# A hybrid encoder layer: x loaded as column blocks and scaled there, its rows' squares taken beside the memory's keys

## The chip, the cores and the metric

One core of a Trainium2 chip runs the whole program in one launch. The metric is the device time of that launch in microseconds. The engines are TensorE (PE; its weight loads are PEld), VectorE (DVE), ScalarE (ACT), GpSimd (POOL) and SyncE (SP), which here only issues DMAs; POOL issues some too.

## What is computed

One encoder layer on x (1024 tokens by 1024), cut to the parts around the change:

```python
h = _rms(x, mix_norm_g)                    # x * rsqrt(mean(x*x) + eps) * g
p = h @ w_in                               # 1952 columns: 256 q, 128 kv, 32 rotary key, 3*512 Hyena
a_out = _mla(p[..., :256], p[..., 256:384], p[..., 384:416], ...)
kf = _hyena_filters(S, ...)                # a small sine net, a window, then a DFT
h_out = _hyena(p[..., 416:], conv_w, conv_b, kf, skip)
x = x + concat(_rms(a_out), _rms(h_out)) @ w_out
x = x + _mem_xattn(_rms(x, cross_norm_g), _rms(mem, mem_norm_g), w_mq, w_mkv, w_mo)
x = x + _hier_moe(...)
return _rms(x, final_norm_g)
```

The change concerns the first two lines, `_rms(x)` and its way into the projection.

## The kernel before

Precision is held by pairs: `split(hi, lo, src)` (L196) casts a tile to fp32r on ACT and subtracts that from the source on DVE, and `mm3` (L206 to L208) makes a product of two such pairs with three matmuls. A matmul contracts over partitions, so the projection needs x with its 1024 columns on partitions, eight blocks of 128, called hA (blocks 0 to 2) and hB (3 to 7), each as a high and a low tile.

The program is written as generators that are advanced in turn, and a scheduler then puts each engine's instructions in one fixed order; an instruction waits in its engine's queue, and all behind it wait with it.

- `spectra` (L286 and on) advances three generators until the filters' spectra are stored. `mem_side` normalises the 256 memory tokens and, for each of 16 column blocks of w_mkv, loads the weights (wm), splits them (wmh, wml), makes 24 matmuls of 256 columns (pmk) and stores the result to DRAM (kvd); later it folds w_mq and w_mo with keys and values. `filter_mlp` is the sine net of two layers (ph, u, h, hh; the cast of its result is h2h). `filters` makes for each of 2 x 8 token blocks a window (dec is the decay table, win the window, eo sums and differences on POOL, L362 and L363, split to eoh and eol), transforms them by DFT tables (ftab, loaded by POOL's DMAs; q1 and q2 are PSUM tiles) and combines them on DVE (L406, kts), which SP stores (Kd).
- `x_rows` comes in when all windows are made. It loads x by rows, eight tiles of 128 tokens (xt, L476), squares each on ACT with a sum (L482), makes the inverse root (`rstd`, L229 to L239: four small DVE operations, and the power on POOL), and scales the row tile by it on ACT (L486). The memory of these tiles was that of the window's tables, so SP's loads wait for the last window activation.
- `in_proj` (L494 and on) turns the rows: `turn_rows` transposes the eight blocks of one row tile on PE into PSUM (pt), and splits them from there into hA and hB. hB lies on memory of the filter transform. Then come twelve columns of 128 (order 8 to 11, then 0 to 7), 48 matmuls each into pu, then ACT (uc, L572) and DVE add the convolution of three taps, and the column is transposed back (pv). `weights` fetches a column's weights one ahead; POOL scales them by the norm's gain gx (L541), ACT casts them (L542), POOL subtracts (L543). From the third column on, the convolution of the finished columns runs between. The last 416 columns (q and kv) take wa, which `split_scaled` (L201, L202) scales and splits.

Tiles of x, of weights and of uc share a pool of eight buffers of 128 x 1024 (`x4`, tag x) and two more (tag u).

## Time and profile before

| | |
|---|---|
| median of 3 runs | 1499.66 us (1496.63 to 1503.1) |
| profiled execution | 1501.6 us, its span 1499.8 us |
| mean granted TensorE clock | 0.969 of full |
| PE / DVE / ACT / POOL busy | 1373.0 / 1034.5 / 701.7 / 498.9 us |

The span runs from the first instruction to the last. A timeline row gives start, duration, engine, line, operation, output and inputs with their shapes, how many equal instructions it joins, and in brackets how long the engine stood idle before it and what it waited for. "x16" in a timeline is one row for sixteen instructions; a DVE or ACT duration contains any time for which the instruction was held up after its start.

### The profile page before, as it was taken

What the parts mean: (1) busy time and instruction counts of PE and PEld (TensorE: products, weight loads), DVE (VectorE), ACT (ScalarE), POOL (GpSimd) and SP (SyncE); (2) the same over time, 40 slices, a digit from 0 to 9 for tenths busy, and PEclk for the clock granted to TensorE, in tenths of its full rate; (3) what the DMA queues carried; (4) which work ended last, traced back from release to release, by engine and by line L of the source; (5) the groups of instructions that cost most, each with busy time, mean ns of one, the idle gap of its engine ahead of it and who ended that gap; (6) DMA issues with size and microseconds to landing.
All of it is one profiled execution on the core that took longest, in us unless ns stands there. A gap on an engine that the chain in (4) does not pass through costs nothing. (4 is left out here: it accounts for less than half of the span.)

```text
span 1499.8 us, 19038 instructions
## 1 busy us (share of the span) xinstructions
PE 1373.0 (92%) x6702; PEld 1025.5 (68%) x6702; DVE 1034.5 (69%) x1755; ACT 701.7 (47%) x1035; POOL 498.9 (33%) x363
## 2 busy tenths in 40 slices
PE   8888988999898989899899999999998999999990
PEld 5777767877787876565555788887886555666660
DVE  7655455389888888456657776434475598899985
ACT  6647446322212224434444344322232687888973
POOL 1321143354433242666666200000001238443322
PEclk9999999999999999999999999999999999999996
DMA  7458776343684525000311421004567899999995
GB/s 266 141 172 298 267 265 224 111 141 130 220 267 154 171 84 168 2 15 1 116 47 43 127 94 57 0 1 169 195 232 253 277 343 362 331 327 331 332 329 216
DMA packets 103406, 272.95 MB, mean 182 GB/s; under 512 B 13162, under 2 KB 41002, under 8 KB 103182
## 3 DMA queue, kind: packets, MB, share of 16 engines
q1 hardware_dynamic: 88590, 222.16, 42.3%
q0 software_dynamic: 14720, 49.57, 11.6%
q8 instruction: 53, 0.87, 0.2%
q14 instruction: 43, 0.35, 0.1%
HBM read 225.83 MB, written 50.07 MB: 184 GB/s over the span
## 5 line engine op out<-in xcount | busy, mean ns | idle before, releaser
L196 DVE TENSOR_TENSOR wt<-raw,wt 128x1024 fp32r<-128x1024 f32 x180 | 214.7, 1217 | 28.1 <-ACT wt L196 25.8
L196 ACT CAST wt<-raw 128x1024 fp32r<-128x1024 f32 x180 | 185.2, 1048 | 20.1 <-PE pgu L208 9.8
L994 POOL TENSOR_TENSOR sums<-sums,e 128x1024 f32<-128x1024 f32 x56 | 134.0, 2393 | 77.2 <-ACT e L990 75.4
L990 ACT ACTIVATE e<-psc 128x1024 f32<-128x1024 f32 x64 | 65.6, 1025 | 85.2 <-PE psc L208 81.9
L950 DVE TENSOR_REDUCE cn<-ptop 128x1 f32<-128x1024 f32 x64 | 75.7, 1211 | 41.2 <-PE ptop L949 40.8
L206 PE MATMUL pgu<-wt,xh 128*80 128x512 f32 x240 | 97.9, 408 | 0.0
L207 PE MATMUL pgu<-wt,xh 128*80 128x512 f32 x240 | 95.5, 398 | 0.0
L208 PE MATMUL pgu<-wt,xh 128*80 128x512 f32 x240 | 95.2, 397 | 0.0
L1835 POOL DMA_INDIRECT acc<-y,tab x28 | 51.2, 1827 | 118.9 <-ACT y L1832 100.7
L206 PE MATMUL psc<-xq,xk 97*128 97x512 f32 (+1 forms) x128 | 56.5, 441 | 11.3 <-ACT e L990 4.5
L1772 POOL DMA_INDIRECT xg<-h3d,tab x32 | 47.6, 1487 | 48.4 <-PE pxt L212 29.3
L999 PE MATMUL po<-e,V 128*64 128x512 f32 x256 | 58.5, 598 | 0.0
L362 POOL TENSOR_TENSOR eo<-win 128x512 f32<-128x512 f32 x16 | 23.8, 1488 | 87.8 <-DVE win L360 87.8
L206 PE MATMUL pw<-woh,ot 128*128 128x512 f32 x128 | 50.6, 395 | 1.6 <-DVE xr L1141 1.3
L207 PE MATMUL psc<-xq,xk 97*128 97x512 f32 (+1 forms) x128 | 52.0, 407 | 0.0
L208 PE MATMUL psc<-xq,xk 97*128 97x512 f32 (+1 forms) x128 | 52.0, 406 | 0.0
L233 POOL TENSOR_TENSOR fr<-fr0v,mhalf 128x1 f32<-128x1 f32 x4 | 2.3, 579 | 149.2 <-DVE fr0v L231 131.1
L572 ACT ACTIVATE uc<-pu,cw 128x1024 f32<-128x1024 f32 x12 | 14.5, 1209 | 78.6 <-PE pu L208 78.6
L206 PE MATMUL pcs<-kh,chh 128*128 128x512 f32 x128 | 50.4, 394 | 0.0
L207 PE MATMUL pw<-wol,ot 128*128 128x512 f32 x128 | 49.9, 390 | 0.0
L208 PE MATMUL pcs<-kh,chl 128*128 128x512 f32 x128 | 49.9, 389 | 0.0
L207 PE MATMUL pcs<-kl,chh 128*128 128x512 f32 x128 | 49.8, 389 | 0.0
(539 smaller groups left out, 4127.3 us busy)
## 6 DMA issues: line engine op xcount, KB each, us to landing
raw<-in_w_exp SPq DMA_DIRECT2D x192, 512.0 KB
tab<-in_t_cfwd POOLq DMA_DIRECT2D x32, 512.0 KB
ftab<-in_t_fwd POOLq DMA_DIRECT2D x16, 768.0 KB
wm<-in_w_mkv SPq DMA_DIRECT2D x16, 512.0 KB
Kd<-kts SPq DMA_DIRECT2D x16, 512.0 KB
kt<-Kd SPq DMA_DIRECT2D x32, 256.0 KB
tab<-in_t_inv SPq DMA_DIRECT2D x32, 256.0 KB
w<-in_w_hy SPq DMA_DIRECT2D x12, 512.0 KB
```

The lines of the kernel that those rows point to most:

```text
L196: return self.nc.scalar.copy(hi, src).ins, self.nc.vector.tensor_tensor(lo, src, hi.bitcast(F32), op=ALU.subtract).ins
L206: mm(out, lh, rh, start=start, stop=False)
L207: mm(out, lh, rl, start=False, stop=False)
L208: mm(out, ll, rh, start=False, stop=stop)
L362: nc.gpsimd.tensor_tensor(t[:, 0], win[:, :512], win[:, 512:], op=ALU.add)
L572: nc.scalar.activation(y, pu, AF.Identity, scale=cw[:, c, 1:2], bias=cw[:, c, 3:4])
L950: nc.vector.tensor_reduce(cn[:, i, r:r + 1], ps, axis=AX.X, op=ALU.max, negate=True)
L990: nc.scalar.activation(e, ps, AF.Exp, scale=SCALE)
L994: nc.gpsimd.tensor_tensor(sums, sums, e, op=ALU.add)
L999: nc.tensor.matmul(po[par * 64:par * 64 + 64], V[:, kt, v], e[:, par * 512:(par + 1) * 512], start=kt == 0, stop=kt == NT - 1, skip_group_ ...
L1772: return nc.gpsimd.indirect_dma_start(out=x, out_offset=None, in_=self.h3d, in_offset=bass.IndirectOffsetOnAxis(ap=tok, axis=0), bounds_ch ...
L1835: scat = nc.gpsimd.indirect_dma_start(out=self.acc, out_offset=bass.IndirectOffsetOnAxis(ap=to, axis=0), in_=y, in_offset=None, bounds_che ...
```

## The change

1. The squares of x's rows move into `mem_side`: in the loop over the 16 memory columns, from c = 5 to 12, one row tile of x is loaded (xq, one more SP DMA of 512 KB each) and, two columns later, squared on ACT. All eight sums go into one tile, and one `rstd` follows at the loop's end (xr_r). `spectra` advances its generators in the same proportion, and `x_rows` two steps at a time.
2. `x_rows` loads x a second time, now as eight column blocks from a transposed copy `xT`, which the host lays out among the inputs. The eight roots per partition are spread over all partitions: DVE multiplies an identity by them (dg), two matmuls in fp32 with a tile of ones sum that over partitions into PSUM (L485), ACT copies it to SBUF (xrb, L486).
3. Each column block is scaled by gx on ACT (L491) and by the roots on POOL (L492), and split into hA or hB from SBUF. Transposes, `turn_rows` and its splits from PSUM are gone.
4. The weights are no longer scaled: L541's multiplication on POOL is gone (ACT's cast is now L541, POOL's subtraction L542), and wa takes `split`, four of 832 columns, in place of eight `split_scaled` of 416.

The diff's core:

```diff
 # spectra
             for step, _ in enumerate(self.filters()):
-                if step % 2 == 0 and not self.made:
+                if not self.made:
+                    if step % 2 == 0:
+                        next(side, None)
                     next(side, None)
-                if not self.made or next(side, self) is not self:
-                    if not self.made:
-                        next(side, None)
                     continue
                 if rows is None:
+                    for _ in side:
+                        pass
                     rows = self.x_rows()
+                next(rows, None)
                 next(rows, None)
...
 # x_rows
+        for k in range(8):
+            t = self.x4([P, S], F32, "xt")
+            nc.sync.dma_start(t, a["xT"][k])
             self.xt.append(t)
...
+        dg, r = self.x4([P, NT, P], F32, "dg", "u"), self.x4([P, S], F32, "xrb", "u")
+        with tc.high_priority():
+            nc.vector.memset(one, 1.0)
+            nc.vector.tensor_tensor(dg, self.ident[:, None, :].broadcast_to([P, NT, P]), self.xr_r[:, :, None].broadcast_to([P, NT, P]), op=ALU.mult)
+            for n in range(2):
+                nc.tensor.matmul(pr[:, n * 512:(n + 1) * 512], one, dg[:, 4 * n:4 * n + 4].rearrange("p i t -> p (i t)"), start=True, stop=True)
+            nc.scalar.copy(r, pr)
...
+        for k in range(8):
+            nc.scalar.activation(self.xt[k], self.xt[k], AF.Identity, scale=self.gx[:, k:k + 1])
+            nc.gpsimd.tensor_tensor(self.xt[k], self.xt[k], r, op=ALU.mult)
+            if k < 3:
+                self.split_x(*self.hA, k, k)
+            if k % 2:
+                yield
...
 # in_proj, weights(c)
-                if "W" in POOL:
-                    nc.gpsimd.tensor_tensor(w, w, self.gx[:, :, None].broadcast_to([P, 8, P]), op=ALU.mult)
-                    nc.scalar.copy(wh, w)
-                    nc.gpsimd.tensor_tensor(wl, w, wh.bitcast(F32), op=ALU.subtract)
+                nc.scalar.copy(wh, w)
+                nc.gpsimd.tensor_tensor(wl, w, wh.bitcast(F32), op=ALU.subtract)
...
             ahead = weights(order[0])
+            for k in range(3, 8):
+                self.split_x(*hB, k - 3, k)
...
-                self.split_scaled(wah[k], wal[k], wa, self.gx[:, 2 * k:2 * k + 2])
+                self.split(wah[k], wal[k], wa)
...
 # mem_side
             for c in range(16):
+                if 5 <= c < 13:
+                    i = c - 5
+                    xs.append((pb.tile([P, D], F32, tag="t4", name="xq", bufs=4), i))
+                if len(xs) > 2 or c > 12 and xs:
+                    x, k = xs.pop(0)
+                    nc.scalar.activation(x, x, AF.Square, accum_out=xss[:, k:k + 1])
                 w = pb.tile([P, 8, P], F32, tag="mw", name="wm")
                 nc.sync.dma_start(w, a["w_mkv"][c])
+                if 5 <= c < 13:
+                    nc.sync.dma_start(xs[-1][0], xv[i // 2, (i % 2) * P:(i % 2 + 1) * P])
...
+            self.xr_r = self.rstd(self.mid, xss, D, "xr")
```

How the change moves instructions, in the order of three engines. In a row stand the line, the operation, output and inputs with the number of the buffer, and the shape.

SP's queue while the first memory columns (wm: weights, kvd: results) are made; before:

```order
L333 DMA skip<-in_hy_skip 1x1024
L244 DMA dec<-in_hy_decay 128x2048
L1219 DMA wm<-in_w_mkv 128x1024 x2
L341 DMA w_520<-in_hy_w 64x1024
L342 DMA w_520<-in_hy_b 1x1024
L1228 DMA kvd<-mko 128x256
L1219 DMA wm<-in_w_mkv 128x1024
L341 DMA w_525<-in_hy_w 64x1024
L1228 DMA kvd<-mko 128x256
L1219 DMA wm<-in_w_mkv 128x1024
```

and with the change, from the same DMA on:

```order
L335 DMA skip<-in_hy_skip 1x1024
L1224 DMA xq<-in_x 128x1024
L1222 DMA wm<-in_w_mkv 128x1024 x2
L1224 DMA xq<-in_x 128x1024 x2
L1222 DMA wm<-in_w_mkv 128x1024
L1233 DMA kvd<-mko 128x256
L1222 DMA wm<-in_w_mkv 128x1024
L1233 DMA kvd<-mko 128x256
L244 DMA dec<-in_hy_decay 128x2048
L1222 DMA wm<-in_w_mkv 128x1024
L1233 DMA kvd<-mko 128x256
```

Three rows of x (xq) now stand between the weights of the first columns; the decay table (dec) and the filter net's last weights (here w_520, its bias, and w_525; w3 in the code) have moved behind them.

DVE from the last windows on, where the last filter transform (q1, q2) ends; before:

```order
L360 TENSOR_TENSOR win_1876<-ph3_1869,win_1876 128x1024
L196 TENSOR_TENSOR eol_1883<-eo_1879,eoh_1882 128x1024
L231 TENSOR_SCALAR xrv_1979<-xss_1976 128x2
L236 TENSOR_TENSOR xrt_1983<-xr_1981 128x2
L237 TENSOR_TENSOR xrt_1983<-xrt_1983,xrv_1979 128x2
L238 TENSOR_SCALAR xrt_1983<-xrt_1983 128x2
L239 TENSOR_TENSOR xr_1981<-xr_1981,xrt_1983 128x2
L406 TENSOR_TENSOR kts_507<-eos_508,q1_1887 128x1024 x2
L231 TENSOR_SCALAR xrv_2021<-xss_2018 128x2
L236 TENSOR_TENSOR xrt_2025<-xr_2023 128x2
L406 TENSOR_TENSOR kts_507<-eos_508,q2_1888 128x1024
L237 TENSOR_TENSOR xrt_2025<-xrt_2025,xrv_2021 128x2
```

and with the change:

```order
L482 MEMSET one_1975 128x128
L396 TENSOR_TENSOR eos_516<-kts_515,pp2_1869 128x1024
L483 TENSOR_TENSOR dg_1977<-ident_66,xr_932 128x1024
L362 TENSOR_TENSOR win_1910<-ph3_1903,win_1910 128x1024
L196 TENSOR_TENSOR eol_1917<-eo_1913,eoh_1916 128x1024
L196 TENSOR_TENSOR hA1_1953<-xt_1959,hA0_1952 128x2x512
L196 TENSOR_TENSOR hA1_1953<-xt_1961,hA0_1952 128x2x512
L408 TENSOR_TENSOR kts_515<-eos_516,q1_1921 128x1024 x2
L196 TENSOR_TENSOR hA1_1953<-xt_1963,hA0_1952 128x2x512
L408 TENSOR_TENSOR kts_515<-eos_516,q2_1922 128x1024 x2
L408 TENSOR_TENSOR kts_515<-eos_516,q1_2038 128x1024 x2
L408 TENSOR_TENSOR kts_515<-eos_516,q2_2039 128x1024
```

The small operations of the roots are gone, a memset and the broadcast's multiplication (dg) stand ahead of the last window, and two subtractions of x (hA1) stand ahead of the first kts, a third behind the first pair. On PE, the second matmul pair of the filter net stands behind one more whole memory column than before, and the two matmuls of L485 behind the first six of q1.

POOL from the last sums and differences of the windows (eo) to the first weights (w_2097 and w_1984 are w8, the first column's); before:

```order
L363 TENSOR_TENSOR eo<-win 128x512
L233 TENSOR_TENSOR xr<-xrv,mhalf 128x2
L375 DMA ftab<-in_t_fwd 128x1536
L233 TENSOR_TENSOR xr<-xrv,mhalf 128x2 x3
L541 TENSOR_TENSOR w_2097<-w_2097,gx 128x1024
L543 TENSOR_TENSOR wl<-w_2097,wh 128x1024
L541 TENSOR_TENSOR w<-w,gx 128x1024
L543 TENSOR_TENSOR wl<-w,wh 128x1024
L766 DMA tab<-in_t_cfwd 128x1024 x5
```

and with the change:

```order
L365 TENSOR_TENSOR eo<-win 128x512
L492 TENSOR_TENSOR xt<-xt,xrb 128x1024 x2
L377 DMA ftab<-in_t_fwd 128x1536
L492 TENSOR_TENSOR xt<-xt,xrb 128x1024 x6
L542 TENSOR_TENSOR wl<-w_1984,wh 128x1024
L542 TENSOR_TENSOR wl<-w,wh 128x1024
L760 DMA tab<-in_t_cfwd 128x1024 x5
L542 TENSOR_TENSOR wl<-w,wh 128x1024 x3
```

Eight multiplications of whole column blocks now follow on each other, with one table's DMA between the second and the third; the weights' multiplication by gx is gone from in front of each subtraction. On PE, the first matmul of the second column's low weights (the wl of the second L542 row) now has 75 matmuls and eight transposes of the first two columns behind it.

## Rows read from the trace of the kernel before

**Rows 1.** The page, busy time, share and instructions of each engine
```profile
PE 1373.0 (92%) x6702; PEld 1025.5 (68%) x6702; DVE 1034.5 (69%) x1755; ACT 701.7 (47%) x1035; POOL 498.9 (33%) x363
```

**Rows 2.** Windows: stretch, length, busy us of PE, PEld, DVE, ACT, POOL, clock, DMA, GB/s
```profile
20.00:40.00 20.00, 19.15 (x132) 15.74 (x132) 18.43 (x28) 17.93 (x23) 0.00 (x0) 1.00 0.59 183
40.00:60.00 20.00, 18.06 (x128) 16.29 (x127) 13.70 (x14) 13.60 (x17) 3.63 (x3) 1.00 0.46 152
```

**Rows 3.** Timeline, DVE and PE, around the hand-over (start, us, engine, line, operation, count, [idle])
```profile
224.31 2.35 DVE L406 TENSOR_TENSOR kts<-eos,q 128x1024 f32<-128x1024 f32 x2 [1.69 <-PE q L208]
...
237.53 0.39 PE L208 MATMUL q<-eoh,ftab 128*128 128x512 f32 x1
237.76 2.20 PE L212 MATMUL pt<-ident,xt 128*128 128x128 f32 x16
...
245.92 0.49 PE L206 MATMUL pu<-hA,wh 128*128 128x512 f32 x1 [0.74 <-ACT hA L196]
```

**Rows 4.** Windows, the same columns, a stretch of columns and convolution
```profile
340.00:380.00 40.00, 36.57 (x187) 30.69 (x185) 36.49 (x51) 6.22 (x9) 17.13 (x12) 1.00 0.45 143
```

**Rows 5.** Instructions by line, ACT on x (count: ns min/median/max, first to last start)
```profile
L482 ACT ACTIVATE xj<-xt x8: 1039/1060/1062, 217.6 to 233.6; 128x1024 f32<-128x1024 f32 x8
L482 ACT ACTIVATION_READ_ACCUMULATOR xj<-xt x8: 183/186/187, 218.5 to 234.5; 128x1 f32 x8
...
L486 ACT ACTIVATE xt<-xt,xr x8: 1132/1137/1157, 222.7 to 237.6; 128x1024 f32<-128x1024 f32 x8
```

**Rows 6.** Timeline, ACT, table load and the filter net's last cast
```profile
22.90 1.28 ACT L281 ACT_TABLE_LOAD   x1
...
45.77 1.05 ACT L196 CAST h2h<-hh 65x1024 fp32r<-65x1024 f32 x1
```

**Rows 7.** Timeline, ACT and PE, first square of x and the last transform's start
```profile
217.55 1.06 ACT L482 ACTIVATE xj<-xt 128x1024 f32<-128x1024 f32 x1 [6.19 <-issue]
...
213.93 0.76 PE L206 MATMUL q<-eoh,ftab 128*128 128x512 f32 x1 [4.49 <-issue]
...
217.91 0.45 PE L206 MATMUL q<-eoh,ftab 128*128 128x512 f32 x1
```

**Rows 8.** Timeline, ACT, ends of the second and third column
```profile
275.48 1.21 ACT L572 ACTIVATE uc<-pu,cw 128x1024 f32<-128x1024 f32 x1 [5.01 <-PE pu L208]
...
287.45 1.21 ACT L572 ACTIVATE uc<-pu,cw 128x1024 f32<-128x1024 f32 x1 [2.87 <-PE pu L208]
```

**Rows 9.** Timeline, PE, matmuls in fp32
```profile
620.87 3.65 PE L999 MATMUL po<-e,V 128*64 128x512 f32 x16
```

**Rows 10.** Instructions by line, POOL, two inputs of 128x1024
```profile
L541 POOL TENSOR_TENSOR w<-w,gx x12: 1895/1902/2342, 236.7 to 449.5; 128x1024 f32<-128x1024 f32 x12
...
L994 POOL TENSOR_TENSOR sums<-sums,e x56: 2348/2386/2725, 612.9 to 832.3; 128x1024 f32<-128x1024 f32 x56
```

**Rows 11.** Timeline, DVE and POOL where both read two SBUF tiles
```profile
104.77 4.89 DVE L196 TENSOR_TENSOR qwl<-qw,qwh 128x1024 fp32r<-128x1024 f32 x1 [2.08 <-ACT qwh L196]
...
104.80 1.28 POOL L363 TENSOR_TENSOR eo<-win 128x512 f32<-128x512 f32 x1
...
345.71 2.61 DVE L805 TENSOR_TENSOR t<-t 128x256 f32<-128x256 f32 x1
...
345.20 2.83 POOL L543 TENSOR_TENSOR wl<-w,wh 128x1024 fp32r<-128x1024 f32 x1
348.00 1.47 POOL L802 TENSOR_TENSOR zj<-fm 128x512 f32<-128x512 f32 x1
```

**Rows 12.** Timeline, DVE, first and last of five long operations, and one alone
```profile
305.59 2.38 DVE L804 TENSOR_TENSOR t<-zj,kt 128x512 f32<-128x512 f32 x1
...
318.53 0.41 DVE L806 TENSOR_TENSOR t<-t 128x256 f32<-128x256 f32 x1
...
402.07 1.57 DVE L806 TENSOR_TENSOR t<-t 128x256 f32<-128x256 f32 x1
```

**Rows 13.** Instructions by line, DVE, the scaled split of wa
```profile
L202 DVE SCALAR_TENSOR_TENSOR wal<-wa,gx,wah x8: 637/640/1666, 478.9 to 492.9; 128x416 fp32r<-128x416 f32 x8
```

More of the change, by code (lines that the diff above doesn't have):

```diff
@@ L470, in x_rows, with split_x @@
         nc.sync.dma_start(self.gx, a["mix_gT"])
-        junk = self.x4([P, D], F32, "xj", "u")
-        xv = a["x"].rearrange("(m r) d -> r m d", r=4)
         self.xt = []
-        for i in range(NT):
-            t = self.x4([P, D], F32, "xt")
-            nc.sync.dma_start(t, xv[i // 2, (i % 2) * P:(i % 2 + 1) * P])
+        for k in range(8):
+            t = self.x4([P, S], F32, "xt")
+            nc.sync.dma_start(t, a["xT"][k])
             self.xt.append(t)
-        yield
-        for i in range(0, NT, 2):
-            ss = pool.tile([P, 2], F32, name="xss")
-            for j in range(2):
-                nc.scalar.activation(junk, self.xt[i + j], AF.Square, accum_out=ss[:, j:j + 1])
-            r = self.rstd(pool, ss, D, "xr")
-            for j in range(2):
-                t = self.xt[i + j]
-                nc.scalar.activation(t, t, AF.Identity, scale=r[:, j:j + 1])
-            yield
+        one = pool.tile([P, P], F32, name="one", bufs=1)
+        pr = self.psum("xr", True)
+        dg, r = self.x4([P, NT, P], F32, "dg", "u"), self.x4([P, S], F32, "xrb", "u")
[5 more added lines that the diff above has]
+            nc.scalar.copy(r, pr)
         self.w8 = self.x4([P, 8, P], F32, "w8", "u")
         nc.sync.dma_start(self.w8, a["w_hy"][8])
+        yield
[5 more added lines that the diff above has]
+            if k % 2:
+                yield
+    def split_x(self, hi, lo, j, k):
+        t = self.xt[k].rearrange("p (n t) -> p n t", n=2)
+        self.turned_x = self.split(hi[:, :, j], lo[:, :, j], t)[1]
     def x4(self, sh, dt, name, tag="x"):
@@ L504, in in_proj @@
             hT = lambda hl, k, cs: (hA[hl] if k < 3 else hB[hl])[:, cs.start // 512, k - 3 * (k > 2), cs.start % 512:(cs.stop - 1) % 512 + 1]
-            def turn_rows(i):
-                pt = self.psum("pt", i % 2 == 0)
-                for k in range(8):
-                    self.transpose(pt[:, k * P:(k + 1) * P], self.xt[i][:, k * P:(k + 1) * P])
-                v, n, ts = pt.rearrange("p (k t) -> p k t", k=8), i // 4, slice(i % 4 * P, i % 4 * P + P)
-                self.split(hA[0][:, n, :, ts], hA[1][:, n, :, ts], v[:, :3])
-                self.turned_x = self.split(hB[0][:, n, :, ts], hB[1][:, n, :, ts], v[:, 3:])[1]
-            for i in range(4):
-                turn_rows(i)
             cw = pa.tile([P, 12, 4], F32, name="cw")
@@ L539, in weights @@
                 wh, wl = self.x4([P, 8, P], F32R, "wh"), self.x4([P, 8, P], F32R, "wl")
-                if "W" in POOL:
-                    nc.gpsimd.tensor_tensor(w, w, self.gx[:, :, None].broadcast_to([P, 8, P]), op=ALU.mult)
-                    nc.scalar.copy(wh, w)
-                    nc.gpsimd.tensor_tensor(wl, w, wh.bitcast(F32), op=ALU.subtract)
-                elif "w" in POOL:
-                    nc.gpsimd.tensor_tensor(w, w, self.gx[:, :, None].broadcast_to([P, 8, P]), op=ALU.mult)
-                    self.split(wh, wl, w)
-                else:
-                    self.split_scaled(wh, wl, w, self.gx)
+                nc.scalar.copy(wh, w)
+                nc.gpsimd.tensor_tensor(wl, w, wh.bitcast(F32), op=ALU.subtract)
                 return wh, wl
@@ L563, in in_proj @@
                         self.mm3(pu[:, ns], wh[:, k], wl[:, k], hT(0, k, ns), hT(1, k, ns), k == 0, k == 7)
-                        if j == 0 and n == 0 and k % 2:
-                            turn_rows(4 + k // 2)
                         if late and k == 7 and (n == 1 or j < 3):
@@ L1216, in mem_side @@
                 yield
+            xv = a["x"].rearrange("(m r) d -> r m d", r=4)
+            xss = self.mid.tile([P, NT], F32, name="xss")
+            xs = []
             for c in range(16):
+                if 5 <= c < 13:
[4 more added lines that the diff above has]
+                    nc.scalar.activation(x, x, AF.Square, accum_out=xss[:, k:k + 1])
                 w = pb.tile([P, 8, P], F32, tag="mw", name="wm")
                 nc.sync.dma_start(w, a["w_mkv"][c])
+                if 5 <= c < 13:
+                    nc.sync.dma_start(xs[-1][0], xv[i // 2, (i % 2) * P:(i % 2 + 1) * P])
                 wh = pb.tile([P, 8, P], F32R, name="wmh")
@@ L2056, in host_arrays @@
     g["x"] = A["x"][0]
+    g["xT"] = A["x"][0][_tok()].T.reshape(8, P, S)
     g["mix_gT"] = A["mix_norm_g"][0].reshape(8, P).T
```

## The prediction

> **What bounds the kernel now.** I read the page first: TensorE is busy for 92% of the span [rows 1], so a gain has to shorten a stretch in which TensorE waits, or take work off it. The change touches three such stretches, and I read each in the windows and the engines' timelines. (A) While the memory's keys are made and the filter net runs, ScalarE and VectorE are nearly full: 17.93 and 18.43 of 20 us between 20 and 40 us, then 13.60 and 13.70 [rows 2]. (B) At 211 us the filters are done, x is loaded, and TensorE finishes the last filter transform; the first eight-block column of the projection begins at 245.92 [rows 3]. (C) From 300 us the projection's columns and the convolution run together, and TensorE has 36.57 and VectorE 36.49 of 40 us [rows 4]: both are at their limit. What I look for is, in each, which wait ends last.
>
> **A, the squares beside the keys: +4 us (0 to +8).** Eight rows of x are now loaded and squared in the loop over the memory's columns. One square is 1.06 us and its read of the sum 0.19 [rows 5], so 10.0 us on ScalarE in all. By the order only three lie in the crowded stretch, 3 x 1.25 = 3.75 us, and two table loads fewer happen there (five before the first forty rows instead of seven), 2 x 1.28 = 2.6 us [rows 6]: a net 1.2 us. The other five lie where ScalarE has 6 us free of 20 [rows 2] and cost nothing; if that cover were gone they would cost 6.2 us. On TensorE's queue the second matmul of the filter net now stands behind a further memory column, 24 matmuls of 256 columns. At full speed the matmuls of 512 columns start 0.23 us apart (237.53 and 237.76 [rows 3]), so 24 x 0.115 = 2.8 us, and that column's weights come behind an x row on SP's queue. 1.2 + 2.8 makes the net's end (the cast of h2h at 45.77 [rows 6]) 4 us later, and I take it that the filters pass this on. Low end 0: TensorE has other memory work to put in. High end 8: the 4 MB of rows, at a DMA share of 0.59 [rows 2], also delay weights by about as much again. The decay table and w3 move back in SP's queue; their readers come after h2h, so I cost this at nothing.
>
> **B, from the load of x to the end of the second column: 0 us (-6 to +12).** The x loads start where they did (the buffers come free with the last window), and the first 512 KB serves ScalarE at 217.55 [rows 7]. What goes: eight squares and eight scalings by the root, 8 x 1.25 + 8 x 1.14 = 19.1 us of ScalarE [rows 5], the small operations of four roots, and 64 transposes on TensorE with their sixteen splits. What comes, in order of the path:
> - ScalarE scales column block 0 by gx, 1.14 [rows 5], and copies the broadcast roots out of PSUM, 1.21 by the nearest row of that shape [rows 8]. The roots' two matmuls in fp32 stand in the trace as two records each; sixteen such take 3.65 us [rows 9], so four take 0.9; they lie ahead of that copy, beside the wait for x. GpSimd can start at 217.55 + 1.14 + 1.21 = 219.9. (Times in this part are those of before, without A's shift.)
> - GpSimd multiplies eight blocks by the roots. No row has this line; the form (two inputs of 128x1024 from SBUF) is that of the softmax sums, 2.39 [rows 10], and the scaling of w by a broadcast gx, 1.90, is the low bound. 8 x 2.39 = 19.1.
> - VectorE's subtraction eol and the three subtractions for hA also read two SBUF tiles, and the trace shows that these and GpSimd's exclude each other. At 345.71 a 0.41 us operation took 2.61, until GpSimd's at 345.20 was done, and got in ahead of GpSimd's next, at 348.00, which took 1.47 [rows 11]: the engine that waits gets in when one instruction ends. So the two alternate. With VectorE's 2.35 / 2 = 1.2 each [rows 3], GpSimd ends at 219.9 + 19.1 + 4 x 1.2 = 243.8.
> - VectorE's order puts two of the hA subtractions ahead of the first kts. Alternating: multiply to 222.3, eol to 223.5, multiply to 225.9, hA to 227.1, multiply to 229.5, hA to 230.7. The kts pair then runs 230.7 to 233.1, and stood at 224.31 to 226.66 before [rows 3]. It frees the PSUM for the second half of the q matmuls: 48 x 0.23 = 11.0 us, so q ends at 244.1 instead of 237.8. This 6.3 us is a new wait of TensorE.
> - hB lies on the filter tables' memory, so its five casts start at 244.1; 5 x 1.05, then the next column's weights 1.05 (the casts of this shape are the h2h row's, 1.05 [rows 6]) and GpSimd's subtraction 2.39 plus one turn of VectorE 1.2: 254.0. By TensorE's order 75 matmuls and eight transposes of the first two columns stand behind that: a column of 48 matmuls and eight transposes takes 287.45 - 275.48 = 11.97 [rows 8], so 75 x 0.23 + 11.97 - 48 x 0.23 = 18.2, and the second column's uc comes at 272.2 instead of 275.48. That is -3.3.
> - After an idle time TensorE was slow: nine matmuls from 213.93, after 4.49 us of waiting, took 3.98 us to the next at 217.91 [rows 7], 0.44 apart instead of 0.23, and 1.9 us were lost. The idle time before 233 is about as long; +2. Some of hB will come later than its matmul; +1, an estimate of one split. Together 0.
>
> Low end -6: no exclusion, q ends where it did, and the transposes' 64 x 2.20 / 16 = 8.8 us [rows 3] are saved by two thirds. High end +12: GpSimd keeps the pair, first rival.
>
> The Trainium skill bears on this in its page SBUF — State Buffer, section "SBUF: two separate sides": the pair of ports that VectorE and GpSimd share is an exclusive lock, held for a whole instruction by whoever starts first, and the other blocks fully. The row at 345.71 agrees; the page does not say who goes next when one engine has a queue of such instructions. The page GPSIMD Engine Reference, section "4.1 Engine selection", speaks against this change: elementwise multiplications belong on VectorE, GpSimd being about twice as slow for two inputs. The rows agree, 2.39 against 1.2; on VectorE the eight would take 9.6 us, and by that the chain above would end some 9 us sooner.
>
> **C, the later columns: -3 us (-9 to 0).** The scaling of w on GpSimd goes, twelve times 1.90 [rows 10], each in front of ScalarE's cast. It also held VectorE: five VectorE operations between 305 and 403 us took 1.57 to 2.38 us where their form takes 0.41 or 0.68 [rows 12], 7.4 us together, while VectorE had nine tenths of the stretch [rows 4]. TensorE has as much to do there, so I let under half reach the path, 3 us. The scaled splits of wa, eight of 0.64 on VectorE [rows 13], become four of 832 columns at about 832/1024 x 1.2 = 1.0: 5.1 to 3.9, no more than 1 us, and a third of it waited for. I take -3 for the two. High end 0: TensorE is the bound; low end -9: all 7.4 and the wa splits' 1.2.
>
> **Sum.** +4 + 0 - 3 = +1, against the profiled execution's own 1501.6 us (span 1499.8): 1502.6. That execution lies 1.9 us above the median of the three runs, 1499.66, so as a median the forecast is 1500.7, and I give **1500.5**. A measurement of this kernel can tell about 0.5% (7.5 us) from no change, so this is no change.
>
> **Rivals.**
> 1. *GpSimd keeps the pair; slower.* At 104.77 a VectorE subtraction of the very form of the hA splits took 4.89 us: it was passed by three GpSimd instructions back to back, the first at 104.80, each 1.28 [rows 11]. The eight multiplications are such a row, since ScalarE's scaling, 1.14, is ahead of them. Then VectorE stands at eol until GpSimd is done at 219.9 + 19.1 = 239.0; eol and two hA subtractions precede the first kts pair, so the q matmuls' second half starts at 239.0 + 3 x 1.2 + 2.35 = 245.0 and ends at 256.0, 12 later than by the alternation. B becomes +12, the sum +13: 1512.7 as a median. It decides if VectorE misses more than two of GpSimd's boundaries on end. For it: that row; against it: the row at 345.71. 0.18.
> 2. *Faster.* The filter net's delay is taken up by memory work (A = 0 or +1), B comes to -5 with little exclusion, and two thirds of C's gain reach TensorE (-6): -10 to -11, or 1489. For it: GpSimd has nothing else there, and both engines stand at nine tenths in C [rows 4]. Against it: TensorE, too, is at nine tenths. 0.26.
> 3. *The squares are not hidden.* The rows of x come ahead of the keys' weights on SP's queue when the DMA share is highest, and TensorE waits for both: A = +10 to +12, the rest as forecast, +7 to +9: 1507 to 1509. Against it: a DMA share of 0.59 and 0.46 after 20 us [rows 2]. 0.10.
>
> **Chances.** My forecast 0.46. Faster by over 0.5% (under 1492): most of rival 2: 0.23. Slower (over 1507): rival 1, half of rival 3 and a little of the forecast's tail: 0.25. Within 0.5%: 0.52. The range goes from rival 2, 1488, to rival 1, 1513, and leaves out the bounds where two of the three parts stand at their ends together. The forecast's own range is 1494 to 1507.
>
> **What would show it.** Right: the cast of h2h some 4 us later; the eight multiplications at L492 of 2.4 us with gaps or lengthenings of 1.2 us, ended near 244; VectorE's subtractions into hA of 2.4 to 3.6 us instead of 1.2; the first kts pair after x near 231 and the last q matmul near 244, with TensorE idle some 6 us ahead of that; the second column's uc at the same distance from the first x load or some us less; no VectorE operation of 1.6 to 2.4 us at L804 to L822. Wrong: an hA subtraction above 5 us (rival 1); the second uc over 8 us nearer to the load of x (rival 2); h2h over 8 us later (rival 3). If the whole differs from the sum of these three stretches, my division is wrong: something behind 560 us has moved that I hold untouched.

## The result, and the profile after

The changed kernel's time is a median of 1511.7 us in eight runs, that of the kernel before 1502.7 in eight runs beside them. The ratio is 1.0051, with an interval of 1.0030 to 1.0072: half a per cent slower, a small difference that is clear of one. One of the changed kernel's eight runs, 1718.5 us at a granted clock of 0.742, counts in its median and not in the ratio; the other seven have a median of 1511.4. The forecast was 1500.5 (1488 to 1513) with no change as the likeliest case. It was counted from the median of three runs of before, 1499.66; from the eight runs' 1502.7 the same +1 us would be 1503.7. The time lies in the range, but two of the three terms of its sum were far off and made up for each other. The profiled execution took 1505.5 us, the fastest of its eight; its span is 3.9 us longer than before's 1499.8. The page of the changed kernel, span and busy time, against [rows 1]:

```profile
span 1503.7 us, 18884 instructions
...
PE 1372.4 (91%) x6642; PEld 1022.5 (68%) x6642; DVE 1033.6 (69%) x1730; ACT 696.9 (46%) x1022; POOL 499.5 (33%) x356
```

Where the 3.9 us come from shows in the start times of the same instructions, of the change minus before (the timelines of DVE and ACT):

| | before, us | change |
|---|---|---|
| split of the last of 16 key columns (DVE wml) | 80.2 | +9.4 |
| last window activation (ACT win) | 210.2 | +12.9 |
| second column's uc (ACT) | 275.5 | +11.7 |
| twelfth column's uc | 473.1 | +7.8 |
| first exponential of the attention (ACT e) | 605.8 | +4.4 |
| span | 1499.8 | +3.9 |

So A is +12.9, B -1.2 and C, with the rest, -7.8. The forecast had +4, 0 and -3.

**A.** Windows of the changed kernel, columns as in [rows 2] and against it; the clock is the figure before the DMA share:

```profile
20.00:40.00 20.00, 17.95 (x113) 14.35 (x112) 16.22 (x23) 14.39 (x21) 0.00 (x0) 0.94 0.79 270
40.00:60.00 20.00, 16.46 (x91) 14.55 (x92) 12.94 (x16) 15.54 (x20) 1.46 (x1) 0.82 0.72 244
```

TensorE's granted clock is 0.82 between 40 and 60 us where it was 1.00, with 91 matmuls instead of 128. From 20 us to the split of the last key column, before and with the change, the windows are:

```profile
20.00:80.21 60.21, 54.20 (x372) 47.92 (x372) 45.80 (x52) 43.07 (x53) 12.86 (x8) 0.97 0.48 155
20.00:89.57 69.57, 59.44 (x370) 51.22 (x370) 50.24 (x57) 50.02 (x68) 16.43 (x9) 0.91 0.61 207
```

For nearly the same matmuls TensorE is busy 5.2 us longer, at a lower clock, and idle 4.1 us longer (10.1 instead of 6.0): these two are the 9.4 us. Shorter windows of the changed kernel:

```profile
50.00:52.00 2.00, 0.71 (x6) 0.50 (x5) 0.00 (x0) 1.99 (x4) 0.00 (x0) 1.00 0.57 154
52.00:54.00 2.00, 1.29 (x4) 1.03 (x5) 1.31 (x2) 2.00 (x3) 0.00 (x0) 0.75 0.96 332
54.00:56.00 2.00, 2.00 (x6) 1.61 (x5) 2.00 (x2) 1.25 (x2) 0.00 (x0) 0.50 1.04 356
60.00:62.00 2.00, 2.00 (x11) 2.00 (x11) 1.31 (x1) 0.07 (x1) 1.90 (x2) 0.50 0.88 311
64.00:66.00 2.00, 2.00 (x19) 2.00 (x18) 1.87 (x2) 1.28 (x3) 2.00 (x2) 1.00 0.20 66
```

In the four us up to 54 TensorE is busy for 2.0; the clock falls between 52 and 54, is 0.50, the lower of its two levels, from 54 to 62, and is back at 1.00 at 64. What it waited for is in the timelines of ACT and PE at that place, against [rows 6]:

```profile
45.46 1.05 ACT L196 CAST wmh<-wm 128x1024 fp32r<-128x1024 f32 x1 [1.75 <-DMA wm<-in_w_mkv]
46.52 1.28 ACT L359 ACT_TABLE_LOAD   x1
...
49.53 1.28 ACT L281 ACT_TABLE_LOAD   x1
...
51.61 1.04 ACT L196 CAST h2h<-hh 65x1024 fp32r<-65x1024 f32 x1
```

```profile
52.71 0.58 PE L206 MATMUL ph<-w3h,h2h 65*128 65x512 f32 x1 [2.00 <-ACT h2h L196]
```

ScalarE waits for a column's weights, then loads the window's table for two activations (0.72 and 0.81 us) and the sine's again before the net's last step, so that h2h comes 5.8 us later and TensorE stands still for it for 2.00 us. After that it works at half its clock. From 52 to 64 us the windows' clock is 0.75, four times 0.50, and 0.69, so 2 x (0.25 + 4 x 0.50 + 0.31) = 5.1 us of full speed are missing, against 9.4 in all; before has a drop of its own near 68 us (0.91 between 60 and 80, 1.8 us). The other 3.5 up to the last window arise at 180 us: the delay is 9.3 at the kts of 172.84 and 12.8 at the window product of 185.99. Timelines of DVE before, and of DVE and PE with the change:

```profile
168.59 1.22 DVE L406 TENSOR_TENSOR kts<-eos,q 128x1024 f32<-128x1024 f32 x1 [1.53 <-DMA Kd<-kts]
```

```profile
180.22 1.22 DVE L408 TENSOR_TENSOR kts<-eos,q 128x1024 f32<-128x1024 f32 x1 [3.30 <-DMA Kd<-kts]
181.35 1.22 DVE L196 TENSOR_TENSOR qwl<-qw,qwh 128x1024 fp32r<-128x1024 f32 x1
```

```profile
182.63 0.76 PE L207 MATMUL pvw<-qwl,kvh 128*128 128x512 f32 x1 [3.29 <-DVE qwl L196]
```

A kts waits 3.30 us for the store of an older one (1.53 before), the split of w_mo's rows stands behind it in VectorE's queue, TensorE waits 3.29 us and then works slowly again, with matmuls 0.43 us apart instead of 0.23 until 185.75.

**B.** Timelines of the hand-over with the change: ACT (the last window, the first scaling of x, the second uc), POOL (the eight multiplications), DVE (eol, two subtractions for hA, the first kts pair), PE (a wait, and the last q matmul), against [rows 3, 7, 8]:

```profile
223.13 1.14 ACT L361 ACTIVATE win<-dec,nt 128x1024 f32<-128x1024 f32 x1
230.10 1.15 ACT L491 ACTIVATE xt<-xt,gx 128x1024 f32<-128x1024 f32 x1 [5.82 <-DMA xt<-in_xT]
...
287.16 1.21 ACT L566 ACTIVATE uc<-pu,cw 128x1024 f32<-128x1024 f32 x1 [5.02 <-PE pu L208]
```

```profile
233.07 5.76 POOL L492 TENSOR_TENSOR xt<-xt,xrb 128x1024 f32<-128x1024 f32 x2 [1.32 <-ACT xrb L486]
...
239.36 16.56 POOL L492 TENSOR_TENSOR xt<-xt,xrb 128x1024 f32<-128x1024 f32 x6
```

```profile
233.97 2.60 DVE L196 TENSOR_TENSOR eol<-eo,eoh 128x1024 fp32r<-128x1024 f32 x1 [4.87 <-ACT eoh L196]
236.60 6.64 DVE L196 TENSOR_TENSOR hA<-xt,hA 128x1024 fp32r<-128x1024 f32 x2
243.16 2.34 DVE L408 TENSOR_TENSOR kts<-eos,q 128x1024 f32<-128x1024 f32 x2
```

```profile
245.61 0.77 PE L206 MATMUL q<-eoh,ftab 128*128 128x512 f32 x1 [4.09 <-issue]
...
258.90 0.39 PE L208 MATMUL q<-eoh,ftab 128*128 128x512 f32 x1
```

Each VectorE subtraction of two SBUF tiles takes 2.6 or 3.3 us instead of 1.2, and each multiplication some 2.8 instead of 2.4 (5.76 for two, 16.56 for six): the two engines alternate, instruction by instruction. TensorE waits 4.09 us, until the first kts pair is done.

**C.** Timelines of POOL and PE in the kernel before, around the sixth column:

```profile
324.05 1.90 POOL L541 TENSOR_TENSOR w<-w,gx 128x1024 f32<-128x1024 f32 x1 [7.87 <-DMA w<-in_w_hy]
327.12 2.41 POOL L543 TENSOR_TENSOR wl<-w,wh 128x1024 fp32r<-128x1024 f32 x1 [1.16 <-ACT wh L542]
329.47 1.65 POOL L766 DMA_DIRECT2D tab<-in_t_cfwd  x3
```

```profile
333.04 0.36 PE L206 MATMUL pf<-zs,tab 128*128 128x256 f32 x1 [2.78 <-issue]
```

The scaling of w (L541), the wait for ScalarE's cast and the subtraction (L543) stand in POOL's queue ahead of three DMAs of the convolution's tables (L766). They are issued from 329.47 on, and TensorE waits 2.78 us for the first. With the change, POOL at the same place:

```profile
335.98 2.71 POOL L542 TENSOR_TENSOR wl<-w,wh 128x1024 fp32r<-128x1024 f32 x1 [10.02 <-ACT wh L541]
339.03 0.56 POOL L760 DMA_DIRECT2D tab<-in_t_cfwd  x1 [0.34 <-PE pf L208]
...
341.90 0.53 POOL L760 DMA_DIRECT2D tab<-in_t_cfwd  x1 [0.90 <-PE pf L208]
```

There is only the subtraction ahead, the tables are issued as TensorE lets their buffers go, and no wait is left. From the fifth uc to the sixth it was 338.6 - 316.4 = 22.2 us, and it is 346.0 - 328.1 = 17.9. The experiments bear this out: it is 17.9 in all nine whose weights POOL doesn't scale, and 23.6, 22.4 and 22.5 in the three that do (e1, e4, e11).

### The profile page after: what moved, and what is told of

The parts are those of the page before. It is cut to its first block, busy times and chain, and to the rows that moved or that the text cites. A ratio compares the mean times of both kernels' runs of the same rounds, so it can differ in the third digit from the quotient of the medians.

```text
span 1503.7 us, 18884 instructions
## 1 busy us (share of the span) xinstructions
PE 1372.4 (91%) x6642; PEld 1022.5 (68%) x6642; DVE 1033.6 (69%) x1730; ACT 696.9 (46%) x1022; POOL 499.5 (33%) x356
## 5 line engine op out<-in xcount | busy, mean ns | idle before, releaser
L1841 POOL DMA_INDIRECT acc<-y,tab x28 | 47.9, 1712 | 117.8 <-ACT y L1838 94.4
L542 POOL TENSOR_TENSOR wl<-w,wh 128x1024 fp32r<-128x1024 f32 x12 | 30.4, 2534 | 74.6 <-ACT wh L541 74.6
L566 ACT ACTIVATE uc<-pu,cw 128x1024 f32<-128x1024 f32 x12 | 14.5, 1207 | 86.2 <-PE pu L208 86.2
L206 PE MATMUL pw<-woh,ot 128*128 128x512 f32 x128 | 51.0, 398 | 1.5 <-DVE xr L1135 1.3
L208 PE MATMUL pw<-woh,ot 128*128 128x512 f32 x128 | 50.2, 393 | 0.0
```

Source lines behind the costliest of these rows:

```text
L206: mm(out, lh, rh, start=start, stop=False)
L208: mm(out, ll, rh, start=False, stop=stop)
L542: nc.gpsimd.tensor_tensor(wl, w, wh.bitcast(F32), op=ALU.subtract)
L1841: scat = nc.gpsimd.indirect_dma_start(out=self.acc, out_offset=bass.IndirectOffsetOnAxis(ap=to, axis=0), in_=y, in_offset=None, bounds_che ...
```

## The experiments

Theory T after the result: the loss is A's, from the rows of x beside the keys, and C gives part of it back. Its rival L had the loss at the hand-over. The table holds all twelve, by the same places as above, in us later than before; the whole is the ratio to before with its 95% interval.

| | last key column | last window | second uc | attention | whole |
|---|---|---|---|---|---|
| the change | +9.4 | +12.9 | +11.7 | +4.4 | 1.0051 (1.0030 to 1.0072) |
| e1 squares early alone | +10.4 | +15.4 | +18.8 | +25.6 | 1.0107 (1.0078 to 1.0136) |
| e2 no squares | +1.6 | +1.9 | +2.2 | -3.0 | 0.9975 (0.9956 to 0.9994) |
| e3 product on VectorE | +10.4 | +15.5 | +12.7 | +12.7 | 1.0036 (1.0011 to 1.0062) |
| e4 gx back on w | +10.2 | +16.3 | +20.7 | +18.1 | 1.0113 (1.0085 to 1.0141) |
| e5 loads only | +8.5 | +8.9 | +9.2 | +7.5 | not to be read |
| e6 squares only | +9.1 | +11.0 | +9.6 | +5.9 | not to be read |
| e7 squares later | +1.7 | +6.0 | +6.7 | +1.8 | 0.9971 (0.9949 to 0.9993) |
| e8 later, VectorE | +1.2 | +4.8 | +2.0 | -1.8 | 0.9978 (0.9953 to 1.0004) |
| e9 from column 8 | +9.3 | +12.5 | +12.8 | +7.8 | 1.0030 (1.0010 to 1.0050) |
| e10 net first | +14.3 | +20.0 | +18.8 | +16.5 | 1.0074 (1.0045 to 1.0102) |
| e11 before, net first | +3.9 | +5.7 | +8.8 | +10.8 | 1.0062 (1.0037 to 1.0087) |
| e12 later, net first | +5.5 | +13.8 | +12.0 | +8.3 | 1.0036 (1.0016 to 1.0056) |

**e1, the squares early, in the kernel before.**

```diff
 # before.py, with the change's mem_side and its order of advancing that; x_rows:
-            ss = pool.tile([P, 2], F32, name="xss")
-                nc.scalar.activation(junk, self.xt[i + j], AF.Square, accum_out=ss[:, j:j + 1])
-            r = self.rstd(pool, ss, D, "xr")
-                nc.scalar.activation(t, t, AF.Identity, scale=r[:, j:j + 1])
+                nc.scalar.activation(t, t, AF.Identity, scale=self.xr_r[:, i + j:i + j + 1])
```

> The kernel before with the first part of the change alone: x's rows are loaded and squared beside the memory's keys, and at x_rows only the scaling by the roots is left (rows, transposes and the scaled weights stay). Theory T (the loss comes from the rows of x beside the keys, 12.9 us by the last window, and the rest of the change gives part of it back): last window activation near 223 us instead of 210, second column's uc near 286 to 288 instead of 275.5, whole run 9 to 13 us slower than before. Rival L (the loss comes from GpSimd's multiplications at the hand-over, and the early delay is made up by then): within 4 us of before, or faster, since ten us of ScalarE's work leave the hand-over.

The early part alone brings the whole delay: T. The run is slower than T said: the hand-over lost 3.4 us more, and in the tenth and eleventh columns TensorE waits up to 4.74 us for a table, as in C. PE's timeline in this kernel:

```profile
480.62 0.36 PE L206 MATMUL pf<-zs,tab 128*128 128x256 f32 x1 [4.74 <-issue]
```

**e2, the rest without the squares.**

```diff
 # after.py, mem_side: no loads of x's rows, no squares
-                    nc.scalar.activation(x, x, AF.Square, accum_out=xss[:, k:k + 1])
+            nc.vector.memset(xss, float(D))
```

> The changed kernel without the early loads and squares of x's rows: the sums are set to a constant, so the norm's roots are left out of the result; all else as changed. Theory T: last window near 210 to 212, second uc near 274 to 276, and the later gain of some 8 us stays: 4 to 10 us faster than before. Rival L: last window near 211, but the second uc 8 to 12 us later than before's 275.5, and the whole 4 to 9 us slower than before.

The early delay is gone, and with it the loss: 1.9 us at the last window, and 0.25% faster as a whole, a little less than T's lower figure. That is what parts 2 to 4 of the change are worth together, as far as a kernel without the norm can show it: tokens may go to other experts here too, but by the first exponential, ahead of the experts, 3.0 us are gained already. Of T's later gain of some 8 us it has 5.2 by then (from +2.2 to -3.0).

**e3, the product on VectorE.**

```diff
-            nc.scalar.activation(self.xt[k], self.xt[k], AF.Identity, scale=self.gx[:, k:k + 1])
-            nc.gpsimd.tensor_tensor(self.xt[k], self.xt[k], r, op=ALU.mult)
+            nc.vector.scalar_tensor_tensor(self.xt[k], self.xt[k], self.gx[:, k:k + 1], r, op0=ALU.mult, op1=ALU.mult)
```

> The changed kernel with the product x times gx times root made in one VectorE instruction for each block, instead of one on ScalarE and one on GpSimd. Theory T: last window near 223 as with the change, hA splits 1.2 us each, the second column's uc within 4 us of the change's 287, whole run within 4 us of the change (6 to 12 us slower than before). Rival L: the second uc 8 to 12 us sooner than with the change, whole run back to before or below it.

From the last window to the second uc it takes 62.5 us, 64.0 with the change. The intervals of the two whole runs overlap; 0.36% is 5 us more than before, a little under T's 6 to 12. GpSimd's slow multiplications cost 1.5 us there, and L falls.

**e4, gx back on the weights.**

```diff
-            nc.scalar.activation(self.xt[k], self.xt[k], AF.Identity, scale=self.gx[:, k:k + 1])
+                nc.gpsimd.tensor_tensor(w, w, self.gx[:, :, None].broadcast_to([P, 8, P]), op=ALU.mult)
-                self.split(wah[k], wal[k], wa)
+                self.split_scaled(wah[k], wal[k], wa, self.gx[:, 2 * k:2 * k + 2])
```

> The changed kernel with gx put back on the weights: GpSimd multiplies each column's weights, wa takes the scaled splits, and x is multiplied by the roots alone. Theory T with the later gain due to the weights: the delay against before stays at 11 to 13 us from the third column to the twelfth instead of falling from 11.7 to 7.8, and the whole is 3 to 8 us slower than with the change. Rival S (the convolution's stretch has slack that makes up any delay): the delay falls as with the change, and the whole is within 2 us of it.

The delay no longer shrinks in the columns (20.7 at the second uc, 22.7 at the twelfth). By itself that would be weak, since in e3, without the scaling, it grows too (12.7 and 14.5); but from the fifth uc to the sixth it is 22.4 us again, so there it was the weights and not slack. The whole is 0.62% above the change, some 9 us, a little over T's 3 to 8; 5.6 of them lie at the hand-over, where the weights' scaling queues behind the eight multiplications (from the last window to the second uc +4.4 instead of -1.2). POOL and PE in this kernel show the wait of before again:

```profile
345.04 1.90 POOL L540 TENSOR_TENSOR w<-w,gx 128x1024 f32<-128x1024 f32 x1 [8.00 <-DMA w<-in_w_hy]
348.10 2.39 POOL L542 TENSOR_TENSOR wl<-w,wh 128x1024 fp32r<-128x1024 f32 x1 [1.16 <-ACT wh L541]
350.43 1.64 POOL L760 DMA_DIRECT2D tab<-in_t_cfwd  x3
```

```profile
354.00 0.36 PE L206 MATMUL pf<-zs,tab 128*128 128x256 f32 x1 [2.84 <-issue]
```

**e5 and e6, loads or squares alone.** Both leave out part of the norm: e5 squares eight numbers of a row, e6 squares the keys' weights instead of x. Tokens then go to other experts, and two more blocks of gathered tokens are worked on at the end, with sixteen more transposes and some 62 us in which TensorE waits for the tokens; so their whole times (1.049 and 1.050 of before) say nothing here, and the places up to the attention do.

```diff
 # e5
-                    nc.scalar.activation(x, x, AF.Square, accum_out=xss[:, k:k + 1])
+                    nc.scalar.activation(x[:, :8], x[:, :8], AF.Square, accum_out=xss[:, k:k + 1])
 # e6: no loads of rows
+                    nc.scalar.activation(x, w.rearrange("p k c -> p (k c)"), AF.Square, accum_out=xss[:, k:k + 1])
```

> The changed kernel with the eight rows of x loaded as with the change, but only the first eight numbers of each row squared: 10 us of ScalarE's work beside the keys go, the 4 MB stay (the norm's sums are left out but for these). Theory D (the delay of 13 us comes from the loads: x rows ahead of the keys' weights on SP's queue): last window still 11 to 16 us later than before's 210.2. Theory Q (it comes from the squares on ScalarE): 2 to 5 us later.

> The changed kernel with eight squares of the keys' weights, which lie in SBUF already, in place of the squares of x's rows, and no loads of rows (the roots are not x's): the 10 us of ScalarE stay, the 4 MB go. Theory D: last window 2 to 5 us later than before's 210.2. Theory Q: 8 to 14 us later.

e6 alone fits theory Q, e5 fits neither: without the squares the last window is 8.9 us late, without the loads 11.0, so the two costs don't add up to the 12.9. At the last key column it is 8.5 and 9.1 against 9.4 with both. e6 is not quite the change without its loads, though: its squares stand ahead of the casts of the same weights, and its tables are loaded in the order of before. What the two have in common with the change is the clock. Windows and PE's longest wait ahead of the drop, of e5 and of e6:

```profile
40.00:60.00 20.00, 16.17 (x89) 14.23 (x89) 13.66 (x17) 14.54 (x18) 0.97 (x1) 0.81 0.64 204
...
54.27 0.51 PE L206 MATMUL ph<-w3h,h2h 65*128 65x512 f32 x1 [2.01 <-ACT h2h L196]
```

```profile
40.00:60.00 20.00, 17.00 (x104) 16.12 (x105) 11.81 (x13) 14.26 (x19) 2.75 (x2) 0.83 0.38 126
...
49.08 0.39 PE L206 MATMUL pmk<-mmh,wmh 128*128 128x256 f32 x1 [1.78 <-ACT wmh L196]
```

Each is enough to make TensorE wait for some weights or for h2h, and the lower clock follows.

**e7, the squares later,** beside the folding of w_mq and w_mo.

```diff
 # mem_side, in the loops that fold w_mq and w_mo, once a step
+            def row():
+                if xs and len(xs) < 9:
+                    x, k = xs.pop()
+                    nc.scalar.activation(x, x, AF.Square, accum_out=xss[:, k:k + 1])
+                if left:
+                    i = left.pop(0)
+                    t = pb.tile([P, D], F32, name="xq")
+                    nc.sync.dma_start(t, xv[i // 2, (i % 2) * P:(i % 2 + 1) * P])
+                    xs.append((t, i))
```

> The changed kernel with the rows of x loaded and squared later, beside the folding of w_mq and w_mo with keys and values (from 80 us on), two row buffers of their own. If the place is what costs: last window 1 to 5 us later than before, whole run between that of the change without squares (0.9975 of before) and before, 1498 to 1506. If the 4 MB cost the same wherever they go, since that stretch too has a DMA share of 0.7 to 0.9: last window 9 us late or more, whole run as with the change.

The keys' loop keeps its clock, and the whole is 0.3% faster than before, the lowest ratio of the versions that compute everything. Some cost remains: the last window is 6.0 us late, a little over the 1 to 5, 4.3 of them after the keys. Windows of this kernel:

```profile
40.00:60.00 20.00, 18.33 (x134) 16.81 (x132) 13.58 (x15) 13.95 (x18) 3.39 (x2) 1.00 0.52 157
```

**e8, that and the product on VectorE.** The edit is that of e3 on e7.

> The last one with the product on VectorE in one instruction for each block as well. If GpSimd's multiplications cost what the experiment with VectorE alone showed (some 2 us of the whole): 1 to 4 us faster than the last one, 0.995 to 1.000 of before. If that was scatter: within 1 us of the last one.

From the last window to the second uc 62.4 instead of 66.0 us, but nothing is left of it in the whole. The two can't be told apart.

**e9, three columns later.**

```diff
-                if 5 <= c < 13:
+                if 8 <= c < 16:
```

> The changed kernel with the loads and squares of x's rows three memory columns later, in columns 8 to 15, so that none stands ahead of the first weights on SP's queue, but two squares still stand ahead of the net's last step on ScalarE. Theory O: h2h 3 to 6 us late, last window 6 to 12 us late. Theory W: as much as with the change, 12 us or more, since all the work is still in the same loop. If only the first loads, ahead of the first weights, cost: last window 0 to 4 us late.

h2h is 2.3 us late and the ninth column too, but the last key column 9.3: the loss comes later in the loop and is as large, and the last window's 12.5 is theory W's. So it is neither the first loads nor h2h as such.

**e10, e11, e12, the net first.**

```diff
-            for _ in mlp:
+            while True:
+                with self.tc.high_priority():
+                    if next(mlp, self) is self:
+                        break
                 next(side, None)
                 next(side, None)
```

> The changed kernel with the filter net's steps given priority in the scheduler: its two layers stand ahead of the memory columns and of the first window on every engine; all loads and squares of x's rows stay beside the keys. Theory O (the early delay is one of order: the net's end comes late, TensorE stands still for it and runs at half its clock after): h2h at 46 us or before, granted clock above 0.95 from 40 to 60 us, last window 1 to 6 us later than before's 210.2, whole run 0.997 to 1.002 of before. Theory W (it is the added work, 4 MB and 10 us of squares, and the order only shows it): last window still 9 to 13 us later, whole run as with the change, 1.004 to 1.008.

> The kernel before with the filter net's steps given the same priority, a control: what that order is worth without the change. Theory O: h2h 3 to 8 us sooner, last window 2 to 8 us sooner, whole run 0.994 to 0.999 of before. If the net's place matters only with the squares: within 0.2% of before.

> The changed kernel with the rows of x loaded and squared beside the folding of w_mq and w_mo (as in the earlier experiment, 0.9971 of before) and the net first. Theory O: 1 to 5 us faster than that experiment, 0.993 to 0.997 of before. If what the net gains is lost again by the last window: as that experiment.

All three contradict theory O: h2h is only 2.1 us late in e10 and 3 us early in the other two, and yet no kernel gains by the edit; e11 is 0.62% slower than before, and e12 lies 0.65% above e7. The rivals don't fit well either: e10's whole is in theory W's range, but its last window is 20.0 us late where W had at most 13, and e11 and e12 were to be as the kernels without the edit. The key columns wait now, and it happens earlier. Windows of e10, and the first of them for e11, against [rows 2]:

```profile
20.00:40.00 20.00, 15.65 (x74) 12.39 (x72) 12.96 (x24) 12.45 (x18) 0.00 (x0) 0.71 0.67 230
40.00:60.00 20.00, 18.55 (x124) 17.46 (x125) 12.30 (x14) 14.87 (x21) 2.47 (x2) 0.91 0.80 248
```

```profile
20.00:40.00 20.00, 15.63 (x78) 12.09 (x77) 15.19 (x27) 9.93 (x13) 0.00 (x0) 0.76 0.42 126
```

While the net's chain runs from ScalarE to VectorE and back, TensorE has no key columns to fill the gaps with. It is busy for 15.6 of 20 us at a clock of 0.71 and 0.76, and does 74 and 78 matmuls instead of 132. In these runs the delay goes not with the end of the net but with TensorE's waits and its clock. Summing (1 - clock) x 20 us over the four windows from 20 to 100 us gives the time lost to the lower clock: 2.6 us before and 1.8 in e2 and e7; 6.4 with the change and in e9, 7.0 in e1, 10.4 in e3, 8.6 in e4, 7.8 in e5, 8.8 in e6, 4.2 in e8, 12.8 in e10, 4.8 in e11 and 8.0 in e12. It goes roughly with the delay of the last key column: against before's 2.6 it is 40 to 75% of the delay in nine of these, all of it in e12, and in e2, e7 and e8, which are 1.2 to 1.7 us late, it is between 0.8 less and 1.6 more. That the clock is a cause and not only a sign is argued from the matmuls' spacing (256 columns in 0.21 us at 60 us, in 0.12 at 64); no run here keeps the waits and holds the clock.

## Why the prediction came out as it did

- **A, the step that failed.** The prediction had +4 and at most +8; it is +12.9 in the profiled execution, and 15.4 to 16.3 in the three other kernels with this early order (e1, e3, e4), which would fit a median 9 us above before's beside a profile only 3.9 above. The step that failed is "1.2 + 2.8 makes the net's end 4 us later, and I take it that the filters pass this on". The net's end was 5.8 late, not far off, but not by these two terms. The net's second matmul, where the 2.8 were put, starts 4.2 us late (25.57, 21.36 before), but its fourth and last of these only 1.1 (38.20, 37.08 before), with as many key matmuls ahead of it as before. From there to h2h it takes 13.4 us instead of 8.7, and this is where most of the 5.8 arise. The squares are not needed for that: e5, with 0.2 us in place of each, has h2h 7.4 us late. What stands in this path had been put at nothing: "The decay table and w3 move back in SP's queue; their readers come after h2h". Their first readers stand ahead of h2h in both kernels. Timelines of ACT before, and of ACT and DVE with the change:

```profile
15.43 1.91 ACT L335 ACTIVATE dec<-dec 128x2048 f32<-128x2048 f32 x1
```

```profile
34.08 1.92 ACT L337 ACTIVATE dec<-dec 128x2048 f32<-128x2048 f32 x1 [1.71 <-DMA dec<-in_hy_decay]
35.90 0.61 ACT L281 ACTIVATE h<-u 64x512 f32<-64x512 f32 x1
...
48.70 0.81 ACT L359 ACTIVATE win<-dec,b,nt 128x512 f32<-128x512 f32 x1
50.82 0.63 ACT L281 ACTIVATE hh<-u 64x512 f32<-64x512 f32 x1
```

```profile
34.00 0.42 DVE L280 TENSOR_SCALAR u<-u 64x512 f32<-64x512 f32 x1
...
42.36 1.21 DVE L196 TENSOR_TENSOR w3l<-w,w3h 65x1024 fp32r<-65x1024 f32 x1
...
48.39 0.42 DVE L280 TENSOR_SCALAR u<-u 64x512 f32<-64x512 f32 x1
```

  With the change ScalarE waits for the table between two steps of the net, and h starts 1.5 us after its input is done. Behind that, w3's split takes 1.2 us of VectorE amid the net's last step, and the first windows, which come late as well (29.85 and 30.73 before), stand with their table loads ahead of hh, which starts 2.0 us after its input is done. TensorE's answer to the waits, some nine us at half clock, was not in the sum either, though part B reckoned with just that; nor was the store of kts at 180 us. And the net's end is not the whole: e9 has the decay table early and h2h 2.3 late, and loses as much. That e5 and e6 bring nearly the same delay shows that such a price isn't a sum of durations.
- **The five squares that "cost nothing".** With the change 7.0 of the 9.4 us are there at the ninth key column, and 2.4 come after it. e9, whose loads and squares all come later, loses 7 us between the ninth column and the last, so there a mean of some 14 of 20 us busy on ScalarE, as before had it, was no cover. What the squares of x cost without their loads no run shows, since e6 squares other data at another place.
- **B was right** at the steps that it named, when counted from the first scaling of x (230.10, 217.55 then). GpSimd's chain ends after 25.8 us (forecast 26.25), the first kts pair starts after 13.1 (13.15), the last q matmul ends after 29.2 (26.55; TensorE is idle for 4.1 us ahead of it where some 6 were forecast, but then the clock is 0.67 between 241.5 and 252), the second uc comes after 57.1 (54.65 and 3 us of reserve). The alternation of VectorE and GpSimd, taken from one row against another [rows 11], held for each of the three operations that had to wait (eol and two for hA).
- **C had the sign right and the reason wrong.** -3 was forecast; from the second uc to the twelfth it is -3.9, and -3.4 more come by the first exponential. Its reason, VectorE held up by GpSimd [rows 12], is not what went: with the change there are still sixteen VectorE operations above 1.4 us between 290 and 440 us, where there were eighteen. What went is the place of L541 in POOL's queue ahead of the tables' DMAs. The prediction counted POOL's queue at the hand-over but not here. Part of this gain is lost again: from the tenth uc to the eleventh the change takes 21.9 us, before 18.1. Apart from e11 no kernel is as short there as before, with the scaling or without; the reason is open. The -3.4 behind the columns are not shown to be the change's. TensorE in the kernel before waits there for a scaled split of wa:

```profile
479.61 0.46 PE L207 MATMUL pq<-wal,hA 128*128 128x416 f32 x1 [2.95 <-DVE wal L202]
```

  With the change the wait is 0.73; but e1 and e4, which keep the scaled splits, make up 4.4 and 4.6 us in the same stretch.
- **Rivals.** GpSimd did not keep the pair (1). Something like the third happened, rows of x not hidden, A of +10 to +12, at a chance of 0.10; its 1507 to 1509 lie below the 1511.7 measured. That the time is in the range is luck: an A three times too small met a gain behind B that is more than twice the -3, nearly half of it in a stretch where the forecast had next to nothing.

The Trainium skill's page SBUF — State Buffer, section "SBUF: two separate sides", says of the shared pair that whoever starts first holds it for a whole instruction. The rows of the hand-over agree, 3.3 us for a subtraction of 1.2; who comes next is not in the page, and here it was the one that had waited. The Trainium skill's page TensorE: Matmul & The Clock Gate, section "Part 1: The HAM clock gate (the "warmup" mystery)", calls the penalty of the ramp, the slow stretch until the clock has first risen, less than 1% of a typical span. No run here shows the ramp by itself. The mean granted clock, 0.966 (0.969 before), holds later drops too, such as the one at 54 us, and 3.8 us more of them between 20 and 100 us go with 9.4 us of delay.

## What to carry to other kernels

Work added beside other work is not free because an engine's mean has room: look at which waits of TensorE it lengthens, and what the granted clock does after them, before summing durations. Where an engine also issues DMAs, an instruction taken off its queue is worth the wait for the transfer behind it, which can be more than the instruction (here 4.3 us for one of 1.90). And when squares of a tensor that is loaded later anyway are to be had early, the place matters more than the work: here 0.8% of the whole, some 12 us, between one loop and the next (1.0051 and 0.9971).

## What the runs showed that was not expected

- The early stretch does worse with its "critical" chain first: the filter net ahead of all else made the kernel before 0.62% slower (1.0037 to 1.0087), with a clock of 0.76 where it was 1.00.
- Loads alone, squares alone (of other data), and both together delay the last key column by 8.5, 9.1 and 9.4 us.
- From the fifth uc to the sixth every kernel takes either 17.9 us or 22.2 to 23.6; what parts the two groups is whether GpSimd scales the weights, 1.90 us in its queue ahead of three table loads.
- Still open: why e7's last window is 6.0 us late when its key columns are only 1.7 late, whether the 4 MB can be placed with no delay at all, why the tenth to the eleventh uc takes longer with the change, and which of the waits between 46 and 54 us it takes to lower the clock.
